# A row gradient of an 8192 x 8192 matrix: 64 successive rows to each partition instead of 256 successive rows to each tile

## The chip, the core and the metric

The kernel runs on one core of a Trainium2 chip. The metric is the device time of one execution in microseconds (us); lower is better.

## What is computed

The input `x` is an 8192 x 8192 matrix of float32, and the output is `np.gradient(x, axis=1)`: along each row, an inner element is half the difference of its right and left neighbours, and the first and the last element are the plain difference of the two elements at that end.

```python
def reference(x: np.ndarray) -> np.ndarray:
    return np.gradient(x, axis=1)     # x: (8192, 8192) float32
```

Rows don't depend on each other, so any row may be worked on in any partition. The whole matrix (268.4 MB) is read once and a result of the same size is written once.

## The kernel before

The on-chip memory has 128 partitions. The kernel takes the matrix in 32 tiles (`nsets`, line 33) of 256 rows; each partition holds `R = 2` rows of a tile side by side, so one partition's part of a tile is 2 x 8192 x 4 bytes = 64 KiB, and it is one contiguous piece of the matrix. Which rows go where is decided by two views, `x_sets` and `out_sets` (lines 36 and 37): in the kernel before, row `(s*128 + p)*2 + t` is row `t` of partition `p` in tile `s`. A tile is therefore 256 successive rows, 8 MiB in one piece, and the parts of two neighbouring partitions lie 64 KiB apart.

There are three buffers, `slots` (line 40), each with room for one tile and 64 elements ahead of it. A tile `i` goes through these steps:

- `load(i)` (line 60): SP, the engine that issues transfers here, starts a DMA from `x_sets[i]` into buffer `i % 3`. From the fourth tile on it first waits until the store that last used that buffer has landed.
- Line 70: GpSimd (POOL) takes the end differences of the two rows, four numbers in each partition, into `ends`.
- Line 76: VectorE (DVE) makes the halved differences of the whole tile in one custom instruction, over 16382 elements in each partition. The output goes into the same buffer, 64 elements further to the front.
- Line 87: GpSimd (for `i % 5` of 1 or 3, but not in the last two tiles) or VectorE puts the four end values into the result. The placing here also overwrites what line 76 wrote where two rows meet.
- Line 89: SP starts the store of the buffer into `out_sets[i]`.

The order is written out by hand under `tc.manual_schedule()`, and `chain` (line 45) keeps only the named dependencies. SP issues three loads at the start. Then each tile's store is issued when the tile is ready, and after every third tile SP issues the next three loads together. All loads and stores go through SP's one queue, so that transfers come in groups of three loads and three stores. No TensorE and no ScalarE work is in the kernel.

Of the kernel before, what the change touches and what calls it, by code (L numbers as in the profile page):

```python
# [1 line left out]

# [4 lines left out]


@with_exitstack
def kernel(  # L10
    ctx: ExitStack,
    tc: tile.TileContext,
    x: bass.AP,
    out: bass.AP,
):

    nc = tc.nc
    P = nc.NUM_PARTITIONS
    n, m = x.shape
    R = 2
    NB = 3  # L30
    SH = 64
    W = R * m
    nsets = n // (P * R)
    f32 = x.dtype

    x_sets = x.rearrange("(s p t) m -> s p (t m)", p=P, t=R)
    out_sets = out.rearrange("(s p t) m -> s p (t m)", p=P, t=R)

    pool = ctx.enter_context(tc.tile_pool(name="pool", bufs=1))
    slots = [pool.tile([P, SH + W], f32, name=f"slot{k}", tag=f"slot{k}") for k in range(NB)]  # L40
    ends = pool.tile([P, nsets, R, 2], f32, name="ends", tag="ends")
    loads, stores = [], [None] * nsets
    in_front = {}

    def chain(i, ins, *needed):

        group, engine = f"slot{i % NB}", ins.ins.engine
        keep = [o.ins for o in needed]  # L50
        if in_front.get(engine, (None,))[0] == group:
            keep.append(in_front[engine][1])
        tc.declare_no_dep(ins.ins, group=group, keep=keep, reason="implied by the needed step")
        tc.add_to_no_dep_group(group, ins.ins)
        in_front[engine] = group, ins.ins
        return ins

    def load(i):
        b = slots[i % NB]
        ins = nc.sync.dma_start(out=b[:, SH : SH + W], in_=x_sets[i])  # L60
        loads.append(chain(i, ins, *([stores[i - NB]] if i >= NB else [])))

    with tc.manual_schedule():
        for i in range(NB):
            load(i)
        for i in range(nsets):
            b = slots[i % NB]
            xin = b[:, SH : SH + W].rearrange("p (t m) -> p t m", m=m)

            ins = nc.gpsimd.tensor_sub(  # L70
                out=ends[:, i, :, :],
                in0=xin[:, :, 1 : m : m - 2],
                in1=xin[:, :, 0 : m - 1 : m - 2],
            )
            at = [chain(i, ins, loads[i])]
            ins = nc.vector._custom_dve(  # L76
                dve_ops.TENSOR_TENSOR_REDUCE_SUB_MAX,
                out=b[:, 1 : W - 1],
                in0=b[:, SH + 2 : SH + W],
                in1=b[:, SH : SH + W - 2],  # L80
                s0=0.0,
                s1=0.5,
            )
            halved = chain(i, ins, *at)
            res = b[:, 0:W].rearrange("p (t m) -> p t m", m=m)
            placer = nc.gpsimd if i % 5 in (1, 3) and i < nsets - 2 else nc.vector
            ins = placer.tensor_copy(out=res[:, :, 0 : m : m - 1], in_=ends[:, i, :, :])  # L87
            placed = chain(i, ins, halved)
            ins = nc.sync.dma_start(out=out_sets[i], in_=b[:, 0:W])
            stores[i] = chain(i, ins, placed)  # L90
            if i % NB == NB - 1:
                for k in range(i + 1, min(i + 1 + NB, nsets)):
                    load(k)


# [1 line left out]
_INS = ['x']  # L97
_OUTS = [((8192, 8192), 'float32')]


# [23 lines left out]
```

## Time and profile before

| What | Value |
|---|---|
| Time, median of 3 runs | 1247.8 us (1247.43 to 1248.43) |
| Profiled execution: its own time | 1247.59 us |
| Profiled execution: span from first to last instruction | 1245.7 us |
| VectorE busy | 554.6 us, 45% of the span |
| GpSimd busy | 8.8 us, 1% of the span |
| Read from and written to HBM | 268.44 MB each |
| Mean rate of all transfers | 431 GB/s |
| Time of the packets of SP's queue, as a share of 16 DMA engines' span | 99.8% |

The profile is one execution of the program, recorded by the hardware profiler. Its page gives busy times of each engine, the span in 40 equal slices with the busy share of each engine in tenths, the transfers by queue, the chain of work that ended last, and the costliest groups of instructions. A transfer is carried out by 16 DMA engines in packets; the page counts the packets and tells how much of the 16 engines' time they took. Times in the views are from the span's start, and the profiled execution's own time is 1.9 us over its span.

### The profile page before, as it was taken

The page shows a single profiled execution, that of the slowest core. Times are in us where ns is not written, and L with a number is a line of the kernel's source. Part 1 is how long each engine was busy: PE and PEld are TensorE (multiplying, and loading weights), DVE is VectorE, ACT ScalarE, POOL GpSimd, SP SyncE. Part 2 cuts the span into 40 slices and gives each one's busy share as a digit, 9 for nine tenths or more (in the row PEclk, how much of TensorE's full clock was granted, in tenths as well). Part 3 has the DMA queues.
Part 4 walks back from the last instruction along what each step waited for, and adds up shares of the span by engine and source line. Part 5 has one row for each costly group of instructions (what it writes and reads, how often), then busy time and mean ns, then how long its engine had stood idle before and what let it go on. Part 6 is the DMA issues. An engine that isn't in the chain of part 4 may idle for free.

```text
span 1245.7 us, 237 instructions
## 1 busy us (share of the span) xinstructions
DVE 554.6 (45%) x52; POOL 8.8 (1%) x48
## 2 busy tenths in 40 slices
DVE  2850583069009702850582079009603840591083
POOL 0000000000000000000000000000000000000000
DMA  9999999999999999999999999999999999999999
GB/s 404 438 436 423 427 431 438 438 438 436 436 427 431 425 438 436 425 434 436 429 434 436 434 436 434 436 434 438 419 436 436 434 438 438 431 434 429 429 410 404
DMA packets 9217, 536.88 MB, mean 431 GB/s; under 512 B 1024, under 2 KB 1024, under 8 KB 1024
## 3 DMA queue, kind: packets, MB, share of 16 engines
q1 hardware_dynamic: 9216, 536.88, 99.8%
q14 instruction: 1, 0.01, 0.0%
HBM read 268.44 MB, written 268.44 MB: 431 GB/s over the span
## 4 chain that ended last, share of the span: by engine, by line
another core or an unknown queue 74%; DVE 18%; DMA 3%; issue 2%; POOL 1%; SPq 0%; POOLq 0%
DVE slot L76 18%; DMA slot<-in_x_dram 3%; POOL ends L70 0%; POOL slot L87 0%; SPq L60 0%; POOLq L119 0%; DVE slot L87 0%
## 5 line engine op out<-in xcount | busy, mean ns | idle before, releaser
L76 DVE CUSTOM_DVE_ANT_0 slot<-slot 128x16382 f32<-128x16382 f32 x32 | 551.2, 17224 | 668.7 <-POOL ends L70 668.7
L70 POOL TENSOR_TENSOR ends<-slot 128x4 f32<-128x4 f32 x32 | 6.3, 198 | 989.6 <-DMA slot<-in_x_dram 989.6
L87 POOL COPY slot<-ends 128x4 f32<-128x4 f32 x12 | 2.3, 190 | 207.9 <-DVE slot L76 207.9
L87 DVE COPY slot<-ends 128x4 f32<-128x4 f32 x20 | 3.4, 172 | 0.7
L108 POOL MEMSET const-bfloat16-1.0<- 128x1 bf16 x1 | 0.1, 101 | 0.0
L108 POOL MEMSET const-uint8-127<- 128x1 uint8 x1 | 0.1, 101 | 0.0
L108 POOL MEMSET const-float32-0.0<- 128x1 f32 x1 | 0.1, 98 | 0.2 <-issue 0.2
L108 POOL MEMSET const-float32-1.0<- 128x1 f32 x1 | 0.1, 98 | 0.0
## 6 DMA issues: line engine op xcount, KB each, us to landing
slot<-in_x_dram SPq DMA_DIRECT2D x32, 58.0
out_dram<-slot SPq DMA_DIRECT2D x32, 40.4
```

The costliest lines, as they stand in the source:

```text
L70: ins = nc.gpsimd.tensor_sub(out=ends[:, i, :, :], in0=xin[:, :, 1 : m : m - 2], in1=xin[:, :, 0 : m - 1 : m - 2],)
L76: ins = nc.vector._custom_dve(dve_ops.TENSOR_TENSOR_REDUCE_SUB_MAX, out=b[:, 1 : W - 1], in0=b[:, SH + 2 : SH + W], in1=b[:, SH : SH + W - 2],
L87: ins = placer.tensor_copy(out=res[:, :, 0 : m : m - 1], in_=ends[:, i, :, :])
L108: nc = _bacc.Bacc("TRN2", target_bir_lowering=False, num_devices=1)
```

## The change

The two views that map rows to tiles and partitions are written with `p` ahead of `s`. In the kernel after, row `p*64 + s*2 + t` is row `t` of partition `p` in tile `s`: each partition works through 64 successive rows of the matrix, two of them in each tile. A partition's part of one tile is still 64 KiB in one piece, but the parts of two neighbouring partitions in a tile now lie 64 rows, 2 MiB, apart, in the input and in the output alike. Nothing else is changed.

```diff
-    x_sets = x.rearrange("(s p t) m -> s p (t m)", p=P, t=R)
-    out_sets = out.rearrange("(s p t) m -> s p (t m)", p=P, t=R)
+    x_sets = x.rearrange("(p s t) m -> s p (t m)", p=P, t=R)
+    out_sets = out.rearrange("(p s t) m -> s p (t m)", p=P, t=R)
```

## The prediction

> **What bounds the kernel now.** I read the head of the page first, then its parts on the slices, the transfers and the groups of instructions.
>
> ```profile
> span 1245.7 us, 237 instructions
> DVE 554.6 (45%) x52; POOL 8.8 (1%) x48
> ...
> DMA  9999999999999999999999999999999999999999
> GB/s 404 438 436 423 427 431 438 438 438 436 436 427 431 425 438 436 425 434 436 429 434 436 434 436 434 436 434 438 419 436 436 434 438 438 431 434 429 429 410 404
> DMA packets 9217, 536.88 MB, mean 431 GB/s; under 512 B 1024, under 2 KB 1024, under 8 KB 1024
> ...
> q1 hardware_dynamic: 9216, 536.88, 99.8%
> ...
> L76 DVE CUSTOM_DVE_ANT_0 slot<-slot 128x16382 f32<-128x16382 f32 x32 | 551.2, 17224 | 668.7 <-POOL ends L70 668.7
> L70 POOL TENSOR_TENSOR ends<-slot 128x4 f32<-128x4 f32 x32 | 6.3, 198 | 989.6 <-DMA slot<-in_x_dram 989.6
> ```
>
> VectorE is busy for 45% of the span, and the DMA row has a 9 in every slice: the kernel is a copy with some arithmetic in its shadow. The idle column of the last two lines says what VectorE waits for: for line 70, and line 70 for the load. The packet line gives the size of what is moved: of 9216 packets of the queue 1024 are tiny, so 8192 carry the 536.88 MB, 65,536 bytes each, which is one partition's part of a tile. Each of the 16 DMA engines has 512 of them to move.
>
> Then I read how the transfers lie in the queue, from the timeline of SP and the waits of SP's queue:
>
> ```profile
> 0.74 1.33 SPq L60 DMA_DIRECT2D slot<-in_x_dram  x3
> 40.40 40.06 SPq L89 DMA_DIRECT2D out_dram<-slot  x3
> 81.78 39.38 SPq L60 DMA_DIRECT2D slot<-in_x_dram  x3
> ```
>
> ```profile
> SPq L89 <- DVE slot L87: 525.6, 20, 55.9
> SPq L60 <- DMA out_dram<-slot: 373.1, 29, 19.3
> ```
>
> SP waits much, but never with an empty queue behind it. The fourth load is issued at 81.78 us, when the first store has landed, and then two more stores are still in the queue; the tile it brings is used at 139.89 us, 58.1 us later, which is three transfers of 19.4 us. So transfers run one after the other, three loads and then three stores, and at any moment all 16 engines read, or all write.
>
> What one packet takes is in the trace's packet records. The median of the 8192 large ones is 2.418 us, for loads and stores alike; a round of 16 packets, one on each engine, starts and ends nearly together. Only 133 packets take over 2.5 us. They are bunched: in four of the 512 rounds all 16 engines are slow, with means of 3.022, 3.515, 2.836 and 3.046 us. The first of these is the first round of the program, and the other three are each the last round of a group of loads, where the stores come behind. The slowest packet takes 3.819 us.
>
> From this the time before can be put together. The packets take 2.426 us in the mean, 512 x 2.426 = 1242.2 us on each engine. Of these 512 x 2.418 = 1238.0 us are the undisturbed packets and the rest is the 133 slow ones (their excess is 61.5 us over 16 engines, 3.8 us). The span has 1245.7 - 1242.2 = 3.5 us beside them (start, last receipt), and the execution's own time 1.9 us more. So **time = 512 x (time of a packet) + 5.4 us**, and the profiled execution's 1247.6 us stands 0.2 us from the median of 1247.8 us. The three runs lie within 0.08% of each other; about 0.2%, 2.5 us, is what can be told from no change.
>
> **The change part by part.** No instruction is added, removed or moved: the two lines change the DRAM addresses of 32 loads and 32 stores. What the compute engines see is the same buffer with other rows of the matrix in it, and rows don't depend on each other. Line 70, 76 and 87 cost nothing more or less: 32 x 17.224 us on VectorE is hidden behind the transfers now and has more cover if they get longer (a tile's three computing steps take 17.9 us from the load's landing to the store's issue, while two other transfers of 19.4 us lie in the queue; only in the last tile is one transfer of cover left, and that is 19.4 us too). The number and the size of packets stay at 8192 and 64 KiB, since each partition's part remains one contiguous piece. SP's issues keep their 0.34 us each, hidden behind the queue.
>
> What is left is the packet's time, and all 512 rounds go through it. Before, the pieces that the engines move at one moment lie within one block of 8 MiB, at steps of 64 KiB or small multiples of it; after, they are spread over the whole 256 MiB of the tensor, at multiples of exactly 2 MiB, the largest power of two that such a layout could get. No packet of the trace of before has such addresses, so I bound the price from both sides. The lower end is 2.418 us, the packet that nothing disturbs: 512 x 2.418 + 5.4 = 1243.4 us, a gain of 4 us, since the most that another layout could give is that the 133 slow packets go. I know of no row that lets a packet be shorter: 2.418 us is the same in loads and stores and in nearly every round, so it looks like a limit of the engine itself. The upper end is the slowest packet, 3.819 us: 512 x 3.819 + 5.4 = 1960.7 us.
>
> Between them I go by the nearest rows, the four rounds in which all 16 engines were held up at once: (3.022 + 3.515 + 2.836 + 3.046) / 4 = 3.105 us. They are the only evidence of what it looks like when the memory and not the engine sets the pace for all 16. With 3.105 us in every round, 512 x 3.105 + 5.4 = 1595.2 us. I take **1595 us**. The extra is 0.687 us over 2.418 us on each packet, 352 us in all less the 3.8 us that are there now. It can't hide: 99.8% of the engines' time is packets, and nothing else is on the path.
>
> The Trainium skill has a rule that speaks against this change. Its page "DMA: Bandwidth & Descriptors", section "Latency and other measured facts", says that when the partitions' rows lie a large power of two apart in HBM, copies get slower: for tiles of 128 partitions x 16 KiB it gives 207 GB/s in each direction at a pitch of 512 KiB, 164 at 2 MiB and 103 at 4 MiB, where 214 is the full rate; it names HBM channels hit by streams in step as an unproved inference. The trace of before has no such pitch; its 431 GB/s agree with the page's full rate (2 x 214). By the page's ratio a packet would be an estimated 2.418 x 214 / 164 = 3.155 us and the time 1621 us, with pieces a quarter of the size of those here.
>
> **The rivals.**
>
> *Part of it.* Engines that collide get out of step, and a 64 KiB packet is long enough to do so; or only one direction suffers. For it: in the trace the slow rounds are never followed by a second fully slow round, the engines recover within one packet. Against it: before, they recover to a layout without a power-of-two distance as wide. If only loads or only stores suffer, 256 rounds x 0.687 us = 176 us, 1423 us. If in each of the 64 transfers only the first two rounds suffer, 128 x 0.687 = 88 us, 1335 us. I give 1250 to 1480 us a chance of 0.25, the upper edge being all rounds at the mean of the 133 slow packets, 2.881 us (512 x 2.881 + 5.4 = 1480).
>
> *No change.* The memory has enough in hand that the spread is not seen at all, and the engine's own 2.418 us remain. For it speaks that the packet times are so even, which shows that the memory is not the limit now, and that the 64 KiB pieces stay whole. Against it speaks that the rounds at 2.8 to 3.5 us show the margin can be used up. Time 1247.6 us, chance 0.09. "HBM Reference", section "Specifications", gives an HBM domain about 716 GB/s; against the 431 GB/s here this would leave a factor of 1.66, and by that figure alone the change would cost nothing.
>
> *Faster.* The slow rounds where loads end and stores begin are the mechanism: tiles that follow one another by 8 MiB before now follow by 64 KiB in every partition, and if that takes the collisions away, the 3.8 us of excess go, and the time is 1243.7 us. To count as faster it must take 2.5 us, two thirds of the excess. Nothing in the profile ties these rounds to addresses. Chance 0.04.
>
> *The change does not do what it says.* If the new views broke the 64 KiB pieces up, the packet count would rise above 9216. Each piece is two whole successive rows in both views, so I give this no chance worth a number.
>
> **How the numbers follow.** The forecast, all rounds slowed to a mean between 2.88 and 3.515 us, has 0.54: 1480 to 512 x 3.515 + 5.4 = 1805 us. Above that, up to 1961 us and beyond, lie 0.08, for rounds worse than the worst of before. With 0.25 for the part, slower by over 0.2% has 0.54 + 0.08 + 0.25 = 0.87, same 0.09, faster 0.04. The range leaves out faster and same (0.13) and some 0.07 above its upper end: from 1255 to 1830 us, which takes in the part and the forecast whole. The likeliest case's own range is 1480 to 1805 us.
>
> **What would show it.** In the profile after: the packet count still 9217, the share of q1 still over 99%, the mean rate down from 431 to about 337 GB/s (536.88 MB over 1593 us), evenly in all 40 slices; VectorE's busy time still 554.6 us, at 35% of the span; the load's landing up from 58.0 to about 3 x 8 x 3.105 = 74.5 us. The packet records should have a median near 3.1 us, in loads and stores. If slices or packets differ between loads and stores, the part is right. A median of 2.418 us would make the forecast wrong, and so would a share of q1 well below 99%, which would mean that the queue runs dry for a reason that I have not seen.

## The result and the profile after

The changed kernel takes 1307.4 us (median of 5 runs, 1306.61 to 1309.37) against 1247.4 us before in the same runs: a ratio of 1.048, interval 1.0469 to 1.0491. It is slower, by 60 us and not by the 347 us forecast. The profiled execution took 1307.45 us at a span of 1305.5 us.

The page of the kernel after, in the same parts as before:

```profile
span 1305.5 us, 237 instructions
...
DVE 554.6 (42%) x52; POOL 8.8 (1%) x48
...
GB/s 353 398 408 382 386 432 428 380 434 426 438 390 434 434 426 402 434 430 396 428 432 434 392 434 434 418 424 422 438 406 430 430 434 416 426 440 420 400 297 295
DMA packets 9217, 536.88 MB, mean 411 GB/s; under 512 B 1024, under 2 KB 1024, under 8 KB 1024
...
q1 hardware_dynamic: 9216, 536.88, 99.1%
...
L76 DVE CUSTOM_DVE_ANT_0 slot<-slot 128x16382 f32<-128x16382 f32 x32 | 551.2, 17223 | 717.6 <-POOL ends L70 717.6
L70 POOL TENSOR_TENSOR ends<-slot 128x4 f32<-128x4 f32 x32 | 6.3, 198 | 1038.5 <-DMA slot<-in_x_dram 1038.5
```

The work is the same: the packets, their bytes and the 554.6 us on VectorE have not changed. Line 70 waits 48.9 us longer for loads (1038.5 against 989.6), so the time was lost in the transfers. The GB/s row tells where. It isn't one lower level: it starts at 353 to 408, then stands near 430 with a dip to 380 to 406 every third or fourth slice, and ends at 297 and 295.

The view by stretches shows these stages; the columns are the stretch, its length, the busy time of VectorE and of GpSimd, PEclk (the clock of TensorE, which has no work here), the DMA share and GB/s. First before, then after:

```profile
2.00:21.00 19.00, 0.00 (x0) 0.00 (x0) 1.00 0.97 414
...
125.00:155.00 30.00, 14.88 (x1) 0.20 (x1) 1.00 0.97 419
274.00:320.00 46.00, 34.62 (x3) 0.58 (x3) 1.00 1.00 433
...
1206.00:1244.00 38.00, 17.40 (x2) 0.20 (x1) 1.00 0.96 414
```

```profile
2.00:21.00 19.00, 0.00 (x0) 0.00 (x0) 1.00 1.01 366
...
125.00:155.00 30.00, 0.00 (x0) 0.00 (x0) 1.00 0.99 343
274.00:320.00 46.00, 35.54 (x4) 0.78 (x4) 1.00 1.00 432
...
1237.00:1256.00 19.00, 17.11 (x3) 0.20 (x1) 1.00 0.56 241
1256.00:1303.00 47.00, 16.81 (x2) 0.00 (x0) 1.00 0.98 335
```

The first load is slow (366 GB/s), the turn from the first three stores to the next three loads is slow (343), a stretch in the middle of later groups is as fast as before (432 and 433), and at the end the engines run half dry for 19 us (DMA share 0.56) and then write the last two tiles at 335 GB/s.

The packet records give the sum. The mean large packet takes 2.525 us (before 2.426), the median is still 2.418. Counting every packet, the 512 rounds lose 55.0 us over that undisturbed value: 10.3 us in the first five transfers, 32.2 us in the ten turns from stores to loads (the last store of a group with the first load of the next; 6.8 us at the first turn, 2.0 at the last; the first turn's store is not among the five), 9.9 us in the last two stores, and 2.6 us elsewhere. Before, it is 4.2 us in all. The engines' idle time between the first and the last packet, in the mean of the 16, rises from 0.6 to 9.2 us. The two increases together, 50.8 + 8.6 = 59.4 us, are nearly the whole of the span's 59.8.

The records also show what the engines do to each other. Following each engine from packet to packet, the n-th packets of the 16 engines start 0.8 to 1.5 us apart in the first rounds, 4.0 us apart after three transfers, and some 19 to 20 us apart in the last loads; in the kernel before they are 0.6 us apart through the first three transfers and 3.0 us in the last loads. And the engines that are ahead at the end find nothing to do: between 1237 and 1254 us up to 15 of the 16 are idle, because SP can issue the store of tile 30 (the next-to-last) only at 1253.6 us, when VectorE has made it:

```profile
1235.89 0.20 POOL L70 TENSOR_TENSOR ends<-slot 128x4 f32<-128x4 f32 x1 [79.08 <-DMA slot<-in_x_dram]
1236.13 17.22 DVE L76 CUSTOM_DVE_ANT_0 slot<-slot 128x16382 f32<-128x16382 f32 x1 [61.85 <-POOL ends L70]
...
1253.58 19.63 SPq L89 DMA_DIRECT2D out_dram<-slot  x2
1255.18 0.20 POOL L70 TENSOR_TENSOR ends<-slot 128x4 f32<-128x4 f32 x1 [19.09 <-DMA slot<-in_x_dram]
```

From 1254.4 us on all 16 start again within 0.4 us, and after a first round at 2.45 us all the rounds of the two last stores take 2.94 to 3.23 us.

### The profile page after: what moved, and what is told of

It reads as the page before. It is cut to its first block, busy times and chain, and to the rows that moved or that the text cites. A ratio compares the mean times of both kernels' runs of the same rounds, so it can differ in the third digit from the quotient of the medians.

```text
span 1305.5 us, 237 instructions
## 1 busy us (share of the span) xinstructions
DVE 554.6 (42%) x52; POOL 8.8 (1%) x48
## 2 busy tenths in 40 slices
DMA packets 9217, 536.88 MB, mean 411 GB/s; under 512 B 1024, under 2 KB 1024, under 8 KB 1024
## 4 chain that ended last, share of the span: by engine, by line
another core or an unknown queue 74%; DVE 17%; DMA 4%; issue 2%; POOL 1%; SPq 0%; POOLq 0%
DVE slot L76 17%; DMA slot<-in_x_dram 4%; POOL ends L70 0%; POOL slot L87 0%; SPq L60 0%; POOLq L119 0%; DVE slot L87 0%
## 5 line engine op out<-in xcount | busy, mean ns | idle before, releaser
L70 POOL TENSOR_TENSOR ends<-slot 128x4 f32<-128x4 f32 x32 | 6.3, 198 | 1038.5 <-DMA slot<-in_x_dram 1038.5
## 6 DMA issues: line engine op xcount, KB each, us to landing
slot<-in_x_dram SPq DMA_DIRECT2D x32, 60.8
```

Source lines behind the costliest of these rows:

```text
L70: ins = nc.gpsimd.tensor_sub(out=ends[:, i, :, :], in0=xin[:, :, 1 : m : m - 2], in1=xin[:, :, 0 : m - 1 : m - 2],)
```

## The experiments

I call the distance between the parts of two neighbouring partitions in DRAM the *pitch*. My theory after reading this was that packets are slow while the engines stand **in step** at addresses that are equal modulo 2 MiB, and that drifting apart cures it. The rivals: the **width** of the spread or the loss of successive pieces costs, not the power of two; certain tiles are slow by their **addresses** alone; the **turn** itself is what costs.

### A pitch that is no power of two

```diff
-    x_sets = x.rearrange("(p s t) m -> s p (t m)", p=P, t=R)
+    last = P * R * (nsets - 1)
+    x_in = x[0:last, :].rearrange("(p s t) m -> s p (t m)", p=P, t=R)
+    x_end = x[last:n, :].rearrange("(p t) m -> p (t m)", t=R)
+    x_sets = [x_in[i] for i in range(nsets - 1)] + [x_end]
...
```

`out_sets` is written in the same way.

> Each partition takes 62 successive rows in the first 31 tiles, and the last tile is the last 256 rows, so neighbouring partitions lie 62 rows (31 x 64 KiB) apart, no power of two, while the spread over the tensor is as wide as in the changed kernel; the result is the same matrix. If the loss comes from partitions lying exactly 2 MiB apart: the loss goes, 1246 to 1252 us, with under 300 packets over 2.5 us. If it comes from the width of the spread alone, or from partitions that do not follow one another in DRAM: 1300 to 1310 us, as changed.

Measured: 1247.5 us, ratio 0.9996 (0.9987 to 1.0006). The page of this kernel:

```profile
GB/s 404 438 438 434 421 425 438 438 438 438 429 436 425 427 438 438 438 438 434 434 436 429 427 434 431 436 438 438 438 436 431 419 432 438 438 434 434 438 387 404
```

The partitions lie 1984 KiB apart instead of 2048, over the same width, and the whole loss is gone. Only 86 packets take over 2.5 us. That rules out the width and the missing succession: what costs is the pitch of 2 MiB. Whether it must be a power of two, or a multiple of a smaller one such as 1.5 MiB costs too, was not tried.

### Letting the engines run dry and start together

The load that waits for the group's last store is issued first, so nothing is in the queue when it starts; the rest of each kernel is unchanged. In the changed kernel and in the kernel before:

```diff
-                for k in range(i + 1, min(i + 1 + NB, nsets)):
+                for k in [k for k in (i + 3, i + 1, i + 2) if k < nsets]:
```

(`loads` becomes a dictionary for it.)

> The changed kernel with the three loads of each group issued in another order, the one that waits for the group's last store first, so that all engines run dry and start again together ten times. In-step theory: each of the ten groups loses what the first six transfers lost in the changed kernel (14 us), instead of 1 to 3 us: 110 to 150 us more than the same reorder costs in the kernel before, 1390 to 1430 us. If only the first tiles and the turns are slow: as much more as the reorder costs in the kernel before (some 20 to 30 us), 1325 to 1340 us.

> The control: the same reorder of loads in the kernel before. Ten gaps of 2 to 3 us in which the engines have nothing to do, and the packets as before: 1268 to 1280 us under every theory, with hardly a slow packet beyond one round for each start.

Measured: 1459.1 us with the changed views (1452.72 to 1466.09; ratio to the kernel before 1.170, 1.165 to 1.174), 1271.6 us with the views of before (ratio 1.019, 1.018 to 1.021). The gaps cost 24 us; the gaps with the pitch of 2 MiB cost 152 us over the changed kernel. The stretches of the second group, three loads and then three stores, first with the views of before, then with the changed ones:

```profile
120.00:178.00 58.00, 16.10 (x1) 0.20 (x1) 1.00 1.01 432
180.00:238.00 58.00, 34.69 (x4) 0.35 (x2) 1.00 1.00 434
```

```profile
130.00:190.00 60.00, 13.69 (x1) 0.20 (x1) 1.00 0.98 404
193.00:268.00 75.00, 35.22 (x5) 0.54 (x3) 1.00 0.96 336
```

The stores run at 336 GB/s all through, where the changed kernel moved the same tiles at 426:

```profile
196.00:250.00 54.00, 17.39 (x2) 0.20 (x1) 1.00 1.02 426
```

The addresses are the same, only the engines' places are not, so addresses alone can't be the cause. The theory held, but my price of 110 to 150 us over the control was low (it is 187 us): I had charged each group as much as the first group of the changed kernel, whose stores began after three loads that had already driven the engines 4 us apart. Here the queue runs dry ahead of the stores as well: in the second group 15 of the 16 engines start their first store between 194.66 and 194.78 us.

### One direction alone

```diff
-    out_sets = out.rearrange("(p s t) m -> s p (t m)", p=P, t=R)
+    out_sets = out.rearrange("(s p t) m -> s p (t m)", p=P, t=R)
```

and for the other run the same with `x_sets`.

> Only the loads have partitions 2 MiB apart; the stores go to 256 successive rows as before, so the output has its rows in another order. In the changed kernel the packets' time over 2.418 us adds up to 24 us of span in loads and 30 us in stores. If each direction loses by itself: 1265 to 1280 us, its slow packets in the loads. If the loss needs both directions (the turns from stores to loads): under 1258 us. If one direction alone does everything: 1300 to 1310 us here or in the other run.

> Only the stores have partitions 2 MiB apart; the loads read 256 successive rows as before, so the output has its rows in another order. If each direction loses by itself: 1270 to 1290 us, its slow packets in the stores, above all the last two. If the loss needs both directions: under 1258 us.

Measured: 1266.0 us with the loads alone (ratio 1.015, 1.013 to 1.017), 1307.5 us with the stores alone (1.050, 1.045 to 1.055). The loads came as expected. The stores cost as much as both together; I had that time only for the case that one direction does everything and the other nothing. The profiled execution of the second is the longest of its runs, 1319.8 us, so I read its stages and not its sum. The stretch with the first three stores, which follow undisturbed loads, and then the three loads behind them:

```profile
63.00:138.00 75.00, 17.09 (x2) 0.00 (x0) 1.00 1.01 328
140.00:200.00 60.00, 34.82 (x4) 0.79 (x4) 1.00 1.00 426
```

The three stores take 3.03, 3.12 and 3.43 us a packet in the mean. In the changed kernel the same three take 2.53, 2.59 and 2.88 us, because the slow loads ahead of them had spread the engines. So the loads' own slowness protects the stores, and the two directions don't add up. The directions differ in how fast they come out of step: with the loads alone, the first load's packets take 2.57 to 3.5 us, and from the second half of the second load on they are mostly under 2.6; the engines are then 2 us apart, at the end of the group 3 us. In the stores alone, the 22 rounds from the first store's second on all take over 2.99 us, while the starts of the 16 engines come apart only from 0.7 to 1.7 us.

### Setting the engines apart from the start

```diff
+        dummies = []
+        for j, k in enumerate((13, 10, 7, 4, 2)):
+            p0, c0 = 64 * (j // 4), SH + 4096 * (j % 4)
+            dummies.append(
+                nc.sync.dma_start(out=slots[2][p0 : p0 + k, c0 : c0 + 4096], in_=x[0:k, 0:4096])
+            )
         for i in range(NB):
             load(i)
...
```

(The load of tile 2 also waits for these small loads.)

> The changed kernel with five small loads ahead of the first one, which write a part of the third buffer that its own load overwrites later; they give some engines up to five packets of 16 KiB more, so that the 16 engines start the first tile up to 3 us apart instead of together. In-step theory (packets are slow while the engines stand at the same place within their 2 MiB, and drift cures it): the first seven transfers lose some 4 us instead of 17, the start costs 3 us, the last two stores stay slow: 1293 to 1302 us. If tiles and turns are slow by their addresses whatever the engines' places: 1308 to 1313 us.

Measured: 1306.3 us (ratio 1.0472, 1.0457 to 1.0488), 1 us less than the changed kernel and outside what I expected of the theory. The records tell why. From 20 to 116 us after the first packet the loss falls from 7.0 to 2.4 us, as it should. In the first load too, once the small loads are through, the packets that start between 10.9 and 20 us take 2.42 us, where those of the changed kernel take 2.96 in the mean. But the first 20 us as a whole lose 3.6 us as they did (3.6 us), with packets up to 7.7 us long beside the small loads, and the first turn (116 to 135 us) still loses 5.8 us (5.4 in the changed kernel); the later turns and the last two stores are as in the changed kernel. Being apart in time helps within a group; it does not save the turn, and the small loads use up some of the gain.

### More turns

One load after each store, in the changed kernel and the kernel before:

```diff
-            if i % NB == NB - 1:
-                for k in range(i + 1, min(i + 1 + NB, nsets)):
-                    load(k)
+            if 1 <= i < nsets - NB + 1:
+                load(i + NB - 1)
```

> The changed kernel with one load issued after each store, in place of three loads after three stores, so that there are 31 turns from stores to loads instead of 10. In the changed kernel a turn loses 5.6 us at first and 2 us late in the run, in its last store and first load. If the turn itself costs: 40 to 60 us over the control's own loss, 1330 to 1370 us. If only engines in step cost, and drift cures that: 1290 to 1310 us.

> The control: one load after each store in the kernel before. In the kernel before a turn from stores to loads loses 0.1 us, and one from loads to stores 0.3 us in the mean: 1246 to 1258 us under every theory, unless the queue runs dry.

Measured: 1357.7 us (1351.86 to 1365.72; ratio 1.089, 1.084 to 1.093) and 1250.9 us (1.0025, 1.0015 to 1.0035). There are 29 turns (not 31, as I had counted), nearly three times as many; they cost 3 us in the layout of before and 50 us on top of the changed kernel, some 2.5 us for each of the 19 more. So there are two losses that both come with the pitch of 2 MiB: starts in step, and turns. In step alone, with drift as its cure, doesn't explain the second: from the middle of this run on the engines end a transfer some 20 us apart, and the turns still cost.

### Smaller pieces

```diff
-        ins = nc.sync.dma_start(out=b[:, SH : SH + W], in_=x_sets[i])
-        loads.append(chain(i, ins, *([stores[i - NB]] if i >= NB else [])))
+        loads.append([])
+        for c in range(0, W, W // 4):
+            ins = nc.sync.dma_start(out=b[:, SH + c : SH + c + W // 4], in_=x_sets[i][:, c : c + W // 4])
+            loads[i].append(chain(i, ins, *(stores[i - NB] if i >= NB else [])))
...
```

The stores are cut in the same way.

> The changed kernel with each load and store in four pieces of 16 KiB for each partition, so that an engine moves through a column strip of 16 KiB at eight partitions before the next strip. In-step theory: a strip is only 0.6 us long, so that engines that have drifted some us apart are still at equal places modulo 2 MiB again and again, and drift cures little: 1350 to 1600 us, a mean packet of 0.65 to 0.8 us where 0.6 us is undisturbed. If the piece does not matter: as changed plus what the control loses, 1300 to 1320 us. By the skill's ratio of 214 to 164: about 1620 us.

> The control: the kernel before with the same four pieces of 16 KiB, where neighbouring partitions lie 64 KiB apart: 1247 to 1265 us, if small packets alone cost little; over 1300 us if the four times as many packets or the number of transfers in flight cost by themselves.

Measured: 1415.2 us (ratio 1.135, 1.132 to 1.137) against 1257.0 us in the control (1.0076, 1.0061 to 1.0091). The mean packet is 0.685 us against 0.613 in the control. In the first store, after eight faster rounds, most rounds of 16 pieces take 0.75 to 0.78 us in the mean, 1.23 to 1.28 times the undisturbed 0.611, about the ratio of 3.03 to 2.418 in stores in step. With short pieces the loss lasts through most of the run and fades only late; the changed kernel with pieces of 16 KiB first, then its control:

```profile
GB/s 378 401 349 321 406 392 354 334 398 391 366 339 406 378 368 347 416 378 361 358 409 378 342 409 403 380 354 423 401 398 381 420 406 373 423 416 413 377 339 323
```

```profile
GB/s 401 421 432 431 429 428 432 432 428 430 431 431 429 430 431 431 429 431 431 430 430 431 430 430 430 433 428 429 431 433 429 429 431 432 429 431 430 432 390 406
```

### A smaller pitch

```diff
+    H = 2
+    x_in = x.rearrange("(h p s t) m -> h s p (t m)", h=H, p=P, t=R)
+    x_sets = [x_in[i * H // nsets, i % (nsets // H)] for i in range(nsets)]
...
```

and `H = 4` for the other; `out_sets` likewise.

> Each partition holds 32 successive rows in each half of the matrix, so neighbouring partitions lie 1 MiB apart. If the loss comes on gradually with the pitch: 1255 to 1290 us. If every large power of two collides alike: about 1307 us. If it takes 2 MiB: 1247 to 1252 us.

> Each partition holds 16 successive rows in each quarter of the matrix, so neighbouring partitions lie 512 KiB apart. If the loss comes on gradually with the pitch: 1248 to 1262 us. If every large power of two collides alike: about 1307 us. If it takes 2 MiB: 1247 to 1249 us.

Measured: 1290.0 us at 1 MiB (ratio 1.035, 1.033 to 1.037) and 1259.9 us at 512 KiB (1.010, 1.008 to 1.011). The loss comes on by degrees: 12 us, 43 us, 60 us at 512 KiB, 1 MiB and 2 MiB. (The smaller pitch also makes the spread narrower; the run at 1984 KiB shows that the width by itself costs nothing.) At 1 MiB the last two stores still take 3.06 and 3.03 us a packet; at 512 KiB they take 2.43 and 2.42.

## Why the prediction was wrong in size

**The bound and what doesn't change** were right. The packet count stayed 9217, VectorE's time 554.6 us at 42% of the span, and 50.8 of the 59.8 us lie in the packets.

**The sign and the cause** were right: partitions 2 MiB apart slow the packets, and no other part of the change costs anything measurable (the run at 1984 KiB). How long the slowness lasts was wrong.

**The term that failed is 3.105 us for all 512 rounds.** The mean measured is 2.525 us. I took the price from four rounds in which all engines were held up. It lies near the 3.03 to 3.43 us of stores in step, but by luck: at 1984 KiB the first round and the last of some groups of loads are slow in the same way (3.02, 3.36 and 2.84 us), with no loss in time, so those rounds have nothing to do with this pitch, and that the memory set their pace was never shown. The error was to hold the price for every round. The same packet records showed that a slow round was never followed by a second slow one, and I set that aside. By the prediction's own test, a median of 2.418 us makes the forecast wrong, and it is 2.418. "Evenly in all 40 slices" and a landing of 74.5 us were wrong with it: the slices go from 295 to 440 GB/s, and the load's median landing is 60.8 us.

**The constant of 5.4 us failed as well.** It is 1307.45 - 1293.0 = 14.4 us. I had written that drawn-out transfers give the computing more cover, even at the last tile. I had also given only the last tile a cover of a single transfer; the next-to-last has no more, since only the last load is in the queue while its 17.7 us of computing run. The engines drifted some 19 us apart, and those ahead ran dry in that time. The tail has 8.3 us of idle time, against 1.6 in the kernel before, and by putting all engines back in step it made the last two stores slow, 9.9 us more.

**The rival "part of it"** had the cause, engines that get out of step, and its chance was 0.25; its price for two slow rounds in each transfer, 1335 us, was nearest to the 1307 measured. The stated range, 1255 to 1830 us, holds the 1307 only because it takes in this rival. What it lacked was where the slow rounds lie: not at the head of each transfer, but at starts in step and at turns. Its other form, one direction alone, gave 1423 us for all rounds of it; the stores alone gave 1307.

**"No change"** assumed that the pitch is not seen at all; it is. **"Faster"** assumed that the slow rounds of before come from the tiles' addresses and would go; they are there at 1984 KiB too, and at 2 MiB the turns got slower.

**The rule of the Trainium skill** ("DMA: Bandwidth & Descriptors", "Latency and other measured facts") was right in direction. Its 164 GB/s in each direction at 2 MiB, 328 in both, is the rate that the in-step stores showed here (328 GB/s in the stretch with the stores alone); the page's copies go from HBM to HBM and here all engines only write, so that the two agree to the digit may be chance. As a price for the whole kernel, an estimated 1621 us, it was far too high, also with pieces of 16 KiB as in its measurement (1415 us, the control at 1257). At 512 KiB its 207 of 214 would be an estimated loss of 3%; here, with pieces of 64 KiB, it was 1.0%. Its account of the cause, streams in step, is an inference on the page. The runs that start the engines together support it, and the pitch of 1984 KiB agrees with it; which part of the memory they collide in, no run here shows.

**What stays open:** why the turn from stores to loads costs more at this pitch (a turn loses under 0.1 us in the kernel before and 1.8 to 6.8 us after) even with engines apart, and why stores keep in step where loads come out of it. The turns are 32.2 of the 55.0 us, so for the larger part of the loss only the pitch is shown as the cause, and not how it acts. No version here beats the kernel before: its packets exceed the undisturbed time by only 4.2 us of 1247, and the pitch of 1984 KiB only equals it.

## What to carry to other kernels

When a transfer-bound kernel maps long runs of rows to partitions, look at the distance between partitions in DRAM: at 512 KiB, 1 MiB and 2 MiB it cost 1.0, 3.5 and 4.8% here with 64 KiB pieces, and 12.6% over its control at 2 MiB with 16 KiB pieces, while 62 rows instead of 64 cost nothing. A price taken from a disturbed packet holds only for as long as the disturbance does, so ask of each slow row in the trace what ended it. And when engines drift, look at the tail: here the queue ran dry for some engines there, and hardly in the middle.

## What the runs showed of the hardware that was not expected

- Engines slowed by equal places modulo 2 MiB come apart by themselves when they load (some 3 us after three transfers with the loads alone), while in stores they stay nearly in step: 22 rounds in a row over 2.99 us against 2.418.
- The loss of the two directions is not a sum: 18.5 us with the loads alone, 60.0 us with the stores alone, 60.0 us with both. Loads that spread the engines make the stores behind them cheaper.
- A turn from stores to loads at this pitch is dear in itself; single packets there took up to 5.5 us in the changed kernel.
